# A decoder layer on one core: the first product in token groups of 256, low weights first in each triple, and three operands of the up product at other addresses

## The chip, the core and the metric

The kernel runs on one core of a Trainium2 chip. The core has five engines that run in parallel, each with a queue of its own that it works through in order: TensorE (PE, with its weight loads listed as PEld), VectorE (DVE), ScalarE (ACT), GpSimd (POOL) and SyncE (SP, which here issues DMAs). They wait for each other through semaphores. Data lies in SBUF (128 partitions), TensorE writes its sums to PSUM banks. The metric is the device time of one execution in microseconds (us); before the change the median of three runs is 1292.92 us (1291.68 to 1296.99).

## The reference

One layer of a decoder on 1024 tokens and 16 meta tokens in front of them, model width 1024, all in float32. Cut to what matters:

```python
h = layer_norm(concat(meta_tokens, x))                 # 1040 x 1024
z = h @ w_in + b_in                                    # the first product
q, k, v, c_in, gates = split(z, [512, 128, 128, 1024, 2048])
y_attn = window_attention(q, k, v) @ w_attn_proj       # 8 query heads, 2 key heads, window 128
c_val, c_gate = split(c_in)
c = causal_dwconv(c_val * sigmoid(c_gate), conv_dw)    # 31 taps, 512 channels
y_conv = silu(layer_norm(c)) @ w_conv_proj
mixed = sigmoid(g_attn) * y_attn + sigmoid(g_conv) * y_conv
h = layer_norm(ALPHA * h + mixed @ w_out)
u, g = split(causal_dwconv(h @ ffn_w_up, ffn_dw))      # 3 taps, 2 x 2816 columns
h = layer_norm(ALPHA * h + (gelu(g) * u) @ ffn_w_down)
return h[16:]                                          # without the meta tokens
```

## The kernel before

Matrix products run in a reduced-width form of float32. So that nothing is lost, each operand is split into a high part (the number rounded to that form, written by a cast) and a low part (the rest, written by a subtraction), and a product of 128 rows is made as a **triple** of matmuls into the same PSUM bank: high weights by high operand, high weights by low operand, low weights by high operand. Each matmul has a weight load of its own. In `product()` these are lines 332, 335 and 336. For the tiles that start the first product `z_first()` has the same triple at line 538, and for up line 1502. The weights of a tile of the first product are loaded (SP), cast on ACT (line 300, `whi`) and split on DVE or POOL (line 303, `wlo`), and both go into buffers of a pool with two of each. A weight tile holds 8 blocks of 128 columns, each block padded to `WS` = 144 floats, so a tile is 1152 floats in a partition, and `wlo` lies 1152 floats behind `whi`.

The stages follow each other in this order (times of the profiled execution):

- **0 to 62 us.** The input norm, and beside it the first three tiles of z (k, v and the first quarter of q).
- **62 to 436.5 us: the first product**, 27 further tiles of 128 columns of z. A tile has the transposed h as the moving operand, its high part in RHO and its low part in RHC. The tokens are cut into the groups of `HG`: 272, 384 and 384 (in the tiles of q and of the gates, which leave out part of the meta tokens, the first group, `TG`, has 258). A group is 8 triples into one of three PSUM banks (`ps_z`), which is then cleared: for the convolution's gate by ACT (lines 689 and 690), for its value by DVE into `cin` (line 697), for the 16 merge gates by ACT (line 713) with a store to DRAM behind it. The first tiles are a pair for the convolution (gate, then value), a second pair, and the rest of q; further pairs and the gates follow, mixed with the attention's small matmuls. DVE runs the 31 taps of the convolution for each pair (lines 704 and 706), beside the attention's softmax. Before the taps DVE copies k (`kx`, line 726 and on), the meta values (`vmT`, `vm`) and v (line 758). When the taps of all four chunks are done, DVE adds them up (`csum`, line 919), PE sums over channels with matmuls on it (`ps_m`, line 924), and DVE does the convolution's layer norm.
- **436.5 to 531 us: the projections** (`ps_p`) of attention and convolution, by `product()`, in groups of 258 and three times 256 tokens (`PG`).
- **531 to 629 us**: the product with w_out, in matmuls of 512 columns.
- **629 to 1062 us: up.** 22 chunks. Each chunk is a two-by-two split of the matrices with seven products instead of eight, on sums of quadrants. The seven operands are B11, B21, BT2, BT1, BT3, BT4 and B22, prepared once and used in all chunks; each product has 12 matmuls over 258 tokens (`SUB` 0) and 12 over 256 (`SUB` 1). `B_AT` says where the operands lie: those over 258 tokens B11 at the start of RHC, B21 4096 floats into RHO, the four BT in OA, and B22 at the start of RX.
- **1062 us to the end**: down, the last norm and the output.

The order of instructions on an engine is made when the kernel is built: a scheduler takes the ready instruction of the lowest rank, with modelled times, and `rank()` gives a stretch of code its rank (evacuations of PSUM have `RK_EVAC`, the splits `RK_SPLIT`). A kernel whose groups or costs change therefore has another order, too. On the chip each engine keeps to its order and waits.

Where tiles lie matters to the text. In lines of 64 bytes from the start of a partition, B11, B21 and B22 over 258 tokens begin at 841.5, 1617.5 and 2920.5; in OA, BT4 begins at 2528 and BT1 at 2268 (multiples of 4 lines, 256 bytes), BT2 at 2138 and BT3 at 2398. The products of a chunk follow as B11 (bank `px`), B21 (`pz`), BT2 (`px`), BT4 (`pw`), BT1 (`py`), BT3 (`px`) and B22 (`py`).

Of the kernel before, what the change touches and what calls it, by code (L numbers as in the profile page):

```python
# [52 lines left out]
HG = [(0, 272), (272, 656), (656, 1040)]  # L53
UG = [(0, 386), (386, 770), (770, 1026)]
# [15 lines left out]
W_FLAT = 96  # L70
# [40 lines left out]
def tile_hybrid_layer(  # L111
# [202 lines left out]
    def weights(shape, fill):  # L314
        fills[0] += 1
        n = fills[0]
        own = n == 3
        raw = OB[:, 0:D].rearrange("p (k c) -> p k c", k=KC) if own else wraw(shape)
        with rank({1: 14, 2: 13, 3: 16, 4: 23}.get(n, RK_SPLIT)):
            last_fill.append(fill(raw))  # L320
        hi, lo = ((sp.tile([P, KC, WS], R, name=t + "3") if own else wsp(t))[:, :, :P] for t in ("whi", "wlo"))
        if n <= 3:
            return hi, lo, raw
        with rank(RK_SPLIT):
            last_split.append(split(raw, hi, lo, n <= 23))
        return hi, lo

    def product(ps, terms, behind=None):

        n = len(terms)  # L330
        for i, (ah, al, bh, bl) in enumerate(terms):
            ins = nc.tensor.matmul(ps, ah, bh, start=i == 0, stop=False)  # L332
            if i == 0 and behind is not None:
                after(ins, behind)
            nc.tensor.matmul(ps, ah, bl, start=False, stop=False)  # L335
            last = nc.tensor.matmul(ps, al, bh, start=False, stop=i == n - 1)  # L336
# [16 lines left out]

    TG = [(a + U0 if i == 0 else a, b) for i, (a, b) in enumerate(HG)]

# [168 lines left out]
    def z_first(g, tiles, *ks, raw=False):  # L524
# [5 lines left out]
        for k in ks:  # L530
            for i in tiles:
# [5 lines left out]
                for j, (w, hl) in enumerate(((hi, 0), (hi, 1), (lo, 0))):  # L537
# [145 lines left out]
    def conv_chunk(c):  # L683
# [8 lines left out]
        z_tile(in_cols(10 + c), HG, g_evac, wt_c1 if c == 1 else None)  # L692
# [6 lines left out]
        z_tile(in_cols(6 + c), HG, v_evac2)  # L699
# [368 lines left out]
    def prep_wo(k, raw=None, behind=None):  # L1068
# [4 lines left out]
        else:  # L1073
            hi, lo = (wsp_flat(n) for n in ("whi", "wlo"))
# [11 lines left out]
    W_AT = (2064, 3088, 0, 1024)  # L1086
# [9 lines left out]
    for m in range(KC):  # L1096
# [42 lines left out]
        if m < 4:  # L1139
            early.append(FA[:, W_AT[m]:W_AT[m] + 1024])  # L1140
            after(load(early[m], w_out_v[m]), last_gate)
# [19 lines left out]
    B_AT = [[(RHC, 0), (RHO, 4096)] + [(OA, OA_UP + i * KC * BS[0]) for i in range(4)] + [(RX, 0)],  # L1161
# [153 lines left out]
    def wsplit(src):  # L1315
# [3 lines left out]
        if RING[i] is None:  # L1319
            RING[i] = wsp_flat(("whi", "wlo")[i % 2])  # L1320
# [328 lines left out]
    def ln_rows():  # L1649
        return [wsp_flat(t, F) for t in ("whi", "wlo")]  # L1650
# [130 lines left out]
```

## Time and profile before

| | us |
|---|---|
| median of three runs | 1292.92 |
| profiled execution | 1290.93 |
| span of it on the core | 1289.1 |
| PE busy | 1263.4 (98%) |
| PE weight loads busy | 1189.8 (92%) |
| DVE busy | 1085.9 (84%) |
| ACT busy | 580.3 (45%) |
| POOL busy | 66.4 (5%) |
| first product, from 62 to | 436.5 |
| up, from 629 to | 1062 |
| mean granted clock of TensorE | 0.995 |

A row of the timeline has the start, the duration, the engine, the line, the operation, what it writes and reads, the shape and how many were put together; in brackets stands how long the engine was idle before it and what ended that. Matmuls are pipelined: a duration reaches over the next one's start, so the pace is read from one start to the next. In a table of stretches each engine's busy time is followed by its count of instructions, and behind POOL's stand the granted clock of TensorE, the busy share of the DMA engines and what they moved. A row of a group has its busy time and the mean in ns of one, and then the idle time ahead of it with what ended most of it.

### The profile page before, as it was taken

To read this page: it belongs to the slowest core of one execution; us is meant where nothing else is said; L and a number is where in the kernel's file an instruction comes from. 1 tells how busy PE (TensorE), PEld (TensorE's weight loads), DVE (VectorE), ACT (ScalarE), POOL (GpSimd) and SP (SyncE) were. 2 spreads that over 40 slices of the span, in tenths; PEclk is the share of its full clock that TensorE was granted. 3 is DMA by queue.
4 is the path that set the end of the run, shared out by engine and by line. 5 is a ranking of instruction groups with operands and counts; after the bars stand their busy time and mean duration, and the time that the engine had idled before them with its cause. 6 is when DMAs were issued, how large, how long until landed. Compare 5 with 4: busy or idle time off the path is not lost.

```text
span 1289.1 us, 21679 instructions
## 1 busy us (share of the span) xinstructions
PE 1263.4 (98%) x8546; PEld 1189.8 (92%) x8546; DVE 1085.9 (84%) x1836; ACT 580.3 (45%) x1051; POOL 66.4 (5%) x35
## 2 busy tenths in 40 slices
PE   7999999999999999999999999999999999999997
PEld 7889999999989999788899999999999997888886
DVE  7888999999967777647899999989899886887697
ACT  5423234454547222344664554555545543536330
POOL 2100000001112222100000000000000000000000
PEclk9999999999999999999999999999999999999999
DMA  6274734334243665222235454453455556989722
GB/s 245 83 265 108 185 93 116 100 82 115 67 112 119 201 166 146 92 82 82 83 103 204 173 208 178 182 202 129 161 182 195 196 198 242 393 286 388 260 76 82
DMA packets 96297, 212.11 MB, mean 165 GB/s; under 512 B 11059, under 2 KB 36211, under 8 KB 95938
## 3 DMA queue, kind: packets, MB, share of 16 engines
q1 hardware_dynamic: 84426, 199.64, 46.2%
q10 hardware_dynamic: 11768, 11.08, 2.6%
q8 instruction: 67, 1.10, 0.4%
q14 instruction: 36, 0.29, 0.1%
HBM read 150.29 MB, written 62.70 MB: 165 GB/s over the span
## 4 chain that ended last, share of the span: by engine, by line
PE 80%; DVE 13%; DMA 4%; ACT 1%; issue 1%; SPq 1%; ACTq 0%; POOL 0%; DVEq 0%
PE px L1502 14%; PE py L1502 9%; PE ps_x L1627 9%; PE ps_z L1627 5%; PE ps_z L332 5%; PE ps_z L335 5%; PE ps_z L336 5%; PE pz L1502 5%; PE pw L1502 5%; DVE FA L706 4%; PE ps_p L336 2%; PE ps_p L335 2%; PE ps_p L332 2%; PE ps_w L332 2%; PE ps_w L336 2%; PE ps_w L335 2%
## 5 line engine op out<-in xcount | busy, mean ns | idle before, releaser
L332 PE MATMUL ps_z<-RHO,whi 128*128 128x384 f32 (+2 forms) x648 | 209.8, 324 | 2.6 <-DVE cin L697 2.6
L335 PE MATMUL ps_z<-RHC,whi 128*128 128x384 f32 (+2 forms) x648 | 210.1, 324 | 0.0
L336 PE MATMUL ps_z<-RHO,wlo 128*128 128x384 f32 (+2 forms) x648 | 209.5, 324 | 0.0
L706 DVE SCALAR_TENSOR_TENSOR FA<-cin,cdw,FA 128x1026 f32<-128x1026 f32 x120 | 154.9, 1305 | 0.1
L332 PEld LDWEIGHTS ps_z<-RHO,whi 128*128 128x128 f32 x648 | 122.5, 189 | 3.5 <-DVE cin L697 3.0
L336 PEld LDWEIGHTS ps_z<-RHO,wlo 128*128 128x128 f32 x648 | 122.3, 189 | 1.2 <-issue 0.3
L335 PEld LDWEIGHTS ps_z<-RHC,whi 128*128 128x128 f32 x648 | 122.6, 189 | 0.7
L300 ACT CAST whi<-wr 128x1024 fp32r<-128x1024 f32 x37 | 38.8, 1049 | 75.6 <-PE ps_z L335 58.4
L1324 DVE TENSOR_TENSOR RHO<-wr,RHO 128x512 fp32r<-128x512 f32 x94 | 64.0, 689 | 9.5 <-ACT RHO L1323 9.5
L1323 ACT CAST RHO<-wr 128x512 fp32r<-128x512 f32 x94 | 56.7, 619 | 25.8 <-DVE wr L1341 11.6
L1341 DVE TENSOR_TENSOR wr<-wr 128x512 f32<-128x512 f32 x88 | 60.6, 689 | 0.2
L303 POOL TENSOR_TENSOR wlo<-wr,whi 128x1024 fp32r<-128x1024 f32 x17 | 42.1, 2474 | 187.2 <-ACT whi L300 158.8
L1514 ACT COPY FA<-px 128x514 f32<-128x514 f32 (+2 forms) x23 | 13.1, 571 | 79.0 <-PE px L1502 79.0
L713 ACT ACTIVATE FA<-ps_z,colr 128x384 f32<-128x384 f32 (+1 forms) x48 | 26.0, 542 | 48.4 <-PE ps_z L336 46.4
L1502 PE MATMUL px<-OA,RHO 128*128 128x258 f32 x324 | 43.2, 282 | 0.0
L1429 ACT ACTIVATE FA<-OB,coll 128x512 f32<-128x512 f32 x44 | 35.9, 816 | 15.2 <-DVE OB L1510 15.2
L1502 PE MATMUL px<-OC,RHO 128*128 128x256 f32 x324 | 42.2, 280 | 0.0
L1502 PE MATMUL px<-RHC,RHO 128*128 128x258 f32 (+1 forms) x312 | 40.9, 280 | 0.4 <-ACT OB L1514 0.4
L1514 ACT COPY OB<-px 128x514 f32<-128x514 f32 (+2 forms) x46 | 26.1, 567 | 32.6 <-PE px L1502 32.6
L1502 PEld LDWEIGHTS px<-OA,RHO 128*128 128x128 f32 x324 | 40.5, 189 | 0.2 <-ACT OB L1514 0.2
L880 ACT ACTIVATE s<-s,sm 128x272 f32<-128x272 f32 (+1 forms) x64 | 31.8, 500 | 18.1 <-DVE sm L876 16.3
L1502 PEld LDWEIGHTS px<-OC,RHO 128*128 128x128 f32 x324 | 39.9, 189 | 0.1
(468 smaller groups left out, 3387.2 us busy)
## 6 DMA issues: line engine op xcount, KB each, us to landing
wr<-in_w_up_dram SPq DMA_DIRECT2D x44, 512.0 KB, 4.2
wr<-in_w_z_dram SPq DMA_DIRECT2D x29, 512.0 KB, 4.0
fd<-FA SPq DMA_DIRECT2D x44, 256.0 KB, 2.5
OB<-in_w_down_dram SPq DMA_DIRECT2D x21, 512.0 KB, 4.7
FA<-sd SPq DMA_DIRECT2D x15, 512.0 KB, 8.1
qt<-qd SPq DMA_DIRECT2D x28, 256.0 KB, 4.0
sgd<-FA ACTq DMA_DIRECT2D x32, 192.0 KB, 2.6
td<-OB SPq DMA_DIRECT2D x12, 512.0 KB, 3.2
```

The costliest lines, as they stand in the source:

```text
L300: ins = nc.scalar.copy(hi, raw)
L303: return (nc.vector if quick else nc.gpsimd).tensor_tensor(lo, raw, f32(hi), OP.subtract)
L332: ins = nc.tensor.matmul(ps, ah, bh, start=i == 0, stop=False)
L335: nc.tensor.matmul(ps, ah, bl, start=False, stop=False)
L336: last = nc.tensor.matmul(ps, al, bh, start=False, stop=i == n - 1)
L706: nc.vector.scalar_tensor_tensor(acc[c], cin[:, j:j + U], wc, acc[c], OP.mult, OP.add)
L1323: nc.scalar.copy(hi, src)
L1324: ins = nc.vector.tensor_tensor(lo, src, f32(hi), OP.subtract)
L1341: ins = nc.vector.tensor_tensor(*x)
L1502: ins = nc.tensor.matmul(o, x[:, ks], bmat(sub, q, hl, k), start=first and k + j == 0, stop=k == 3 and j == 2, skip_group_check=not first)
L1514: copied.append(nc.scalar.copy(*x))
L1627: nc.tensor.matmul(banks[i], l[:, ts], r[:, ws], start=first and a and x + k == 0, stop=z and x == len(ops) - 1 and k == 2, skip_group_che ...
```

## The change

Four things are changed together.

1. The 27 later tiles of the first product use `ZG`: token groups of 272 (258 in q and the gates), 256, 256 and 256 instead of 272, 384 and 384. The starting tiles keep `HG`. A group is cleared as before, so each tile has one more clearing, and a merge gate one more store.
2. The triple of `product()` and of `z_first()` begins with low weights by high operand, then high by high, then high by low. Up keeps its order.
3. `whi` and `wlo` become one tile `w` of 2304 floats (pool of two); the low part begins 1136 instead of 1152 floats behind the high one, 64 bytes lower, in the padding behind the last block of the high part. The flat views that later stages take of these buffers have the addresses that they had.
4. Three operands of up over 258 tokens move: B11 by 40 floats, B21 by 40 floats and B22 by 56 floats. They then begin at lines 844, 1620 and 2924.

The rename of `W_AT` to `E_AT` in the w_out stage only frees the name. With item 3's line numbers, 332, 335 and 336 become 341, 342 and 338; 300 and 303 become 302 and 305, 697 becomes 703, 713 becomes 719, 919 and 924 become 925 and 930.

```diff
+ZG = [(0, 272), (272, 528), (528, 784), (784, 1040)]
...
-W_FLAT = 96
+W_AT = (0, 1136)
+W_FLAT = (96, 1136 + 112)
...
-    def wsp(tag, dtype=R):
-        return wsp_p.tile([P, KC, WS], dtype, name=tag, tag=tag)
-
-    def wsp_flat(tag, dtype=R):
-        return wsp(tag, dtype).rearrange("p k c -> p (k c)")[:, W_FLAT:W_FLAT + D]
+    def chunks(t):
+        return [t[:, o:o + KC * WS].rearrange("p (k c) -> p k c", k=KC)[:, :, :P] for o in W_AT]
+
+    def wsp(dtype=R):
+        return wsp_p.tile([P, 2 * KC * WS], dtype, name="w", tag="w")
+
+    def wsp_flat(dtype=R):
+        t = wsp(dtype)
+        return [t[:, o:o + D] for o in W_FLAT]
...
-        hi, lo = ((sp.tile([P, KC, WS], R, name=t + "3") if own else wsp(t))[:, :, :P] for t in ("whi", "wlo"))
+        hi, lo = chunks(sp.tile([P, 2 * KC * WS], R, name="w3") if own else wsp())
...
-            ins = nc.tensor.matmul(ps, ah, bh, start=i == 0, stop=False)
+            ins = nc.tensor.matmul(ps, al, bh, start=i == 0, stop=False)
...
-            nc.tensor.matmul(ps, ah, bl, start=False, stop=False)
-            last = nc.tensor.matmul(ps, al, bh, start=False, stop=i == n - 1)
+            nc.tensor.matmul(ps, ah, bh, start=False, stop=False)
+            last = nc.tensor.matmul(ps, ah, bl, start=False, stop=i == n - 1)
...
-    TG = [(a + U0 if i == 0 else a, b) for i, (a, b) in enumerate(HG)]
+    TG = [(a + U0 if i == 0 else a, b) for i, (a, b) in enumerate(ZG)]
...
-                for j, (w, hl) in enumerate(((hi, 0), (hi, 1), (lo, 0))):
+                for j, (w, hl) in enumerate(((lo, 0), (hi, 0), (hi, 1))):
...
-        z_tile(in_cols(10 + c), HG, g_evac, wt_c1 if c == 1 else None)
+        z_tile(in_cols(10 + c), ZG, g_evac, wt_c1 if c == 1 else None)
...
-        z_tile(in_cols(6 + c), HG, v_evac2)
+        z_tile(in_cols(6 + c), ZG, v_evac2)
...
-    B_AT = [[(RHC, 0), (RHO, 4096)] + [(OA, OA_UP + i * KC * BS[0]) for i in range(4)] + [(RX, 0)],
+    B_AT = [[(RHC, 40), (RHO, 4096 + 40)] + [(OA, OA_UP + i * KC * BS[0]) for i in range(4)] + [(RX, 56)],
             [(OC, OC_UP + i * 2048) for i in range(4)] + [(RHC, 4096 + R_DN), (RHC, 2048 + R_DN), (RHC, 6144 + R_DN)]]
```

More of the change, by code (lines that the diff above doesn't have):

```diff
@@ L1073, in prep_wo @@
         else:
-            hi, lo = (wsp_flat(n) for n in ("whi", "wlo"))
+            hi, lo = wsp_flat()
         if raw is None:
@@ L1085, in tile_hybrid_layer @@
     GS += [(OB, i * 516) for i in range(5)]
-    W_AT = (2064, 3088, 0, 1024)
+    E_AT = (2064, 3088, 0, 1024)
     def gslot():
@@ L1139, in tile_hybrid_layer @@
         if m < 4:
-            early.append(FA[:, W_AT[m]:W_AT[m] + 1024])
+            early.append(FA[:, E_AT[m]:E_AT[m] + 1024])
             after(load(early[m], w_out_v[m]), last_gate)
@@ L1319, in wsplit @@
         if RING[i] is None:
-            RING[i] = wsp_flat(("whi", "wlo")[i % 2])
+            RING[i:i + 2] = wsp_flat()
         t = RING[i]
@@ L1649, in ln_rows @@
     def ln_rows():
-        return [wsp_flat(t, F) for t in ("whi", "wlo")]
+        return wsp_flat(F)
     gains = ln_rows()
```

## The prediction

> **What bounds the kernel now.** I read the busy table first, then the stretches, then the chain of work that ended last. TensorE (PE) is busy 98% of the span, so its own pace and its few waits set the time; but in the first product (62 to 436.5 us) VectorE (DVE) is nearly as full:
>
> ```profile
> PE 1263.4 (98%) x8546; PEld 1189.8 (92%) x8546; DVE 1085.9 (84%) x1836; ACT 580.3 (45%) x1051; POOL 66.4 (5%) x35
> ```
> ```profile
> core 0: us, PE busy (x) PEld busy (x) DVE busy (x) ACT busy (x) POOL busy (x), PEclk, DMA share, GB/s
> 86.00:94.00 8.00, 5.37 (x29) 5.05 (x28) 5.98 (x17) 1.04 (x1) 0.00 (x0) 0.79 0.74 272
> 118.00:215.00 97.00, 95.10 (x622) 94.08 (x622) 90.60 (x152) 34.69 (x84) 0.00 (x0) 1.00 0.48 129
> ...
> 300.00:364.00 64.00, 62.62 (x403) 59.99 (x401) 63.60 (x119) 33.16 (x87) 9.62 (x4) 1.00 0.29 84
> 364.00:436.50 72.50, 72.37 (x444) 70.87 (x445) 53.60 (x108) 36.51 (x59) 12.21 (x5) 1.00 0.50 140
> ```
>
> So there are two questions: what the change does to the pace of the matmuls, and whether DVE lets the first product use it. The pace is read from starts. In the timeline of PE, 5 steps of 272 columns lie between the first two rows below (0.63 us, 126 ns each), 26 of 384 from there to the next (4.52 us, 173.8 ns each), and 22 of 384 between the last two (3.92 us, 178.2 ns each): the same product has two paces.
>
> ```profile
> 64.81 0.29 PE L335 MATMUL ps_z<-RHC,whi 128*128 128x272 f32 x1
> ...
> 65.44 0.34 PE L332 MATMUL ps_z<-RHO,whi 128*128 128x384 f32 x1
> ...
> 69.96 0.34 PE L336 MATMUL ps_z<-RHO,wlo 128*128 128x384 f32 x1
> ...
> 118.01 0.34 PE L336 MATMUL ps_z<-RHO,wlo 128*128 128x384 f32 x1
> ...
> 121.93 0.34 PE L332 MATMUL ps_z<-RHO,whi 128*128 128x384 f32 x1
> ```
>
> 256 columns have two paces as well, at the start of up, where pieces of 12 follow each other without a break:
>
> ```profile
> 629.11 1.58 PE L1502 MATMUL px<-OC,RHO 128*128 128x256 f32 x12
> 630.53 1.58 PE L1502 MATMUL pz<-OC,RHO 128*128 128x256 f32 x12
> 631.94 1.58 PE L1502 MATMUL px<-OC,RHO 128*128 128x256 f32 x12
> ...
> 635.55 1.65 PE L1502 MATMUL pw<-RHC,RHO 128*128 128x256 f32 x12 [0.97 <-ACT FA L1304]
> 637.03 1.52 PE L1502 MATMUL py<-OC,whi 128*128 128x256 f32 x12
> 638.39 1.52 PE L1502 MATMUL px<-RHC,wlo 128*128 128x256 f32 x12
> ```
>
> Between 629.11 and 631.94 lie 24 matmuls: 117.9 ns each. Behind a wait of 0.97 us it is 1.36 us for 12: 113.3 ns. These operands all stand to their weights in the same way in memory (the next weights begin 64 bytes behind the operand, taken modulo 256), so with one placement both paces occur, and the pace seems to be carried on from what ran before. In the projections, 72 steps of 256 columns lie between these two rows, 117.1 ns each:
>
> ```profile
> 450.95 0.29 PE L332 MATMUL ps_p<-OA,whi 128*128 128x256 f32 x1
> ...
> 459.38 0.28 PE L332 MATMUL ps_p<-OA,whi 128*128 128x258 f32 x1
> ```
>
> **The up product.** The chain of waits shows seven products of up in a row (the first closes one chunk, six belong to the next), each 12 matmuls of 258 and 12 of 256 columns (start, us, what):
>
> ```profile
> 946.66 2.86 PE py L1502 x24
> 949.52 2.85 PE px L1502 x24
> 952.37 2.85 PE pz L1502 x24
> 955.22 2.81 PE px L1502 x24
> 958.03 2.81 PE pw L1502 x24
> 960.85 2.81 PE py L1502 x24
> 963.66 2.81 PE px L1502 x24
> ```
>
> The first three are those of B22, B11 and B21, the three operands that are moved; the other four read OA. The moved ones lie half a 64-byte line off a line; among the four, those of pw and py lie on multiples of 256 bytes. After the change the three lie on such multiples too. Were they then to run as pw and py do, they would lose 0.05 + 0.04 + 0.04 = 0.13 us a chunk, times 22 chunks: **-2.9 us**. PE has no wait here that could hide it: it is what the chain runs along. Bounds: nothing changes (0); or the half-line cost is paid in another form. The best 256-column pace, 113.3 against 117.9 ns, bounds the gain: 36 x 4.6 ns x 22 = -3.6. A loss is not excluded by a row; the same 0.13 a chunk the other way, +2.9, bounds it. I take -2.9, since the four products on lines all run at 2.81.
>
> **The first product: more and smaller groups.** Each of the 27 tiles that come after the start has 1040 or 1026 columns; two groups of 384 become three of 256, for 24 matmuls each, so 48 matmuls become 72 in a tile, 648 more in all. What the order does, on PE at the edge of the first two groups, before:
>
> ```order
> L336 MATMUL ps_z<-RHO,wlo 128x272
> L332 MATMUL ps_z<-RHO,whi 128x384
> L335 MATMUL ps_z<-RHC,whi 128x384
> L336 MATMUL ps_z<-RHO,wlo 128x384
> L332 MATMUL ps_z<-RHO,whi 128x384
> ```
>
> and after:
>
> ```order
> L342 MATMUL ps_z<-RHC,w 128x272
> L338 MATMUL ps_z<-RHO,w 128x256
> L341 MATMUL ps_z<-RHO,w 128x256
> L342 MATMUL ps_z<-RHC,w 128x256
> L338 MATMUL ps_z<-RHO,w 128x256
> ```
>
> The low weights have moved ahead of the two high ones. With lo one line lower, every weight load now begins 64 bytes behind the operand being read (modulo 256); before, one in three began 128 behind. That is the placement of the 629 us rows, so 113.3 or 117.9 ns are the prices. A pair of 384s takes 347.6 to 356.4 ns, three 256s 339.9 to 353.7. Times 648: from -10.7 to +4.0 us; the middles (352.0 and 346.8) give **-3.4** of PE work. The same order and placement hold for the 576 matmuls of 256 columns of the projections, at 117.1 now: -2.2 to +0.5, taken as **-0.9**, the middle; they lie on the path (PE 94.5 of 94.5 us from 436.5 to 531).
>
> A rule speaks against all of this. The Trainium skill, "TensorE: Matmul & The Clock Gate", Part 1, "Wait — 56ns, not 53.3ns?", has a fixed cost of about 2.5 ns for each matmul and nothing that depends on addresses; by it 648 matmuls cost 1.6 us more, an estimate from that page, and the moves nothing. The trace disagrees: one size has two paces, 113.3 and 117.9 ns.
>
> **The first product: a wait that goes.** At 86 us PE stands still, the largest wait that it has:
>
> ```profile
> 86.41 0.34 PE L336 MATMUL ps_z<-RHO,wlo 128*128 128x384 f32 x1
> 89.38 0.59 PE L332 MATMUL ps_z<-RHO,whi 128*128 128x272 f32 x1 [2.63 <-DVE cin L697]
> ...
> 92.49 0.41 PE L335 MATMUL ps_z<-RHC,whi 128*128 128x272 f32 x1
> ```
> ```profile
> 86.61 1.04 ACT L300 CAST whi<-wr 128x1024 fp32r<-128x1024 f32 x1 [10.62 <-PE ps_z L335]
> ```
> ```profile
> 87.69 1.23 DVE L303 TENSOR_TENSOR wlo<-wr,whi 128x1024 fp32r<-128x1024 f32 x1 [4.98 <-ACT whi L300]
> 88.83 1.55 DVE L697 SCALAR_TENSOR_TENSOR cin<-ps_z,colr,FA 128x272 f32<-128x272 f32 x3
> ...
> 100.17 0.28 DVE L748 TENSOR_TENSOR vm<-ps_vm,vm 64x128 fp32r<-64x128 f32 x1 [2.71 <-ACT vm L747]
> ...
> 104.08 1.22 DVE L303 TENSOR_TENSOR wlo<-wr,whi 128x1024 fp32r<-128x1024 f32 x1 [2.08 <-ACT whi L300]
> 105.23 0.81 DVE L704 TENSOR_SCALAR FA<-cin,cdw,colr 128x1026 f32<-128x1026 f32 x1
> ```
>
> DVE waits at L303 for a cast on ACT, which waits for a weight buffer that PE still reads; the three evacuations of PE's banks (L697) stand behind L303. PE waits 2.6 us for a bank, and then runs at half pace: from 89.38 to 92.49 lie 13 steps of 239 ns, against 126 for 272 columns at 65 us, 1.5 us more (granted clock 0.79 in 86 to 94). On DVE, before:
>
> ```order
> L303 TENSOR_TENSOR wlo<-wr,whi 128x8x128
> L697 SCALAR_TENSOR_TENSOR cin<-ps_z,colr,FA 128x272
> L697 SCALAR_TENSOR_TENSOR cin<-ps_z,colr,FA 128x384 x2
> L726 CAST kx_758<-FA 128x8x128
> L726 CAST kx_758<-FA 128x8x16
> ```
>
> and after, the end of the same stretch, behind three evacuations that now come early:
>
> ```order
> L748 COPY vmT<-FA 64x16 x4
> L703 SCALAR_TENSOR_TENSOR cin<-ps_z,colr,FA 128x256
> L305 TENSOR_TENSOR w<-wr,w 128x8x128
> L754 TENSOR_TENSOR vm<-ps_vm,vm 64x2x64
> L764 TENSOR_TENSOR v<-ps_v_794,v 128x4x64 x2
> ```
>
> This split (now L305) has sunk from ahead of the evacuations to behind all four, so the circle of waits opens. The fourth evacuation is queued behind the work on kx and vmT; the tile's next user of that bank comes three groups on, so I leave PE about 1 us of wait there (an estimate: some 7 us of kx and vmT work from 90.29 on against two groups of 2.8). On PE that is 2.6 + 1.5 - 1.0, a gain of **3.1 us**. DVE's three waits above add up to 9.8 us; I let 1.8 stand, so DVE reaches the first tap of the convolution (L704) about 8 us sooner.
>
> **What the first product can keep.** From that tap on DVE carries the taps (L706) and the attention until csum, for which PE waits:
>
> ```profile
> 361.11 2.96 DVE L919 TENSOR_TENSOR csum<-csum,FA 128x1026 f32<-128x1026 f32 x1
> ```
> ```profile
> 362.41 0.28 PE L335 MATMUL ps_z<-RHC,whi 128*128 128x258 f32 x1
> 364.13 1.35 PE L924 MATMUL ps_m<-csum,ones 128*128 128x386 f32 x4 [1.44 <-DVE csum L919]
> ...
> 436.65 0.28 PE L332 MATMUL ps_p<-OA,whi 128*128 128x258 f32 x1
> ```
>
> PE's order puts a fixed amount of the product behind csum, so the product's end is csum plus 72 us. On PE there, before:
>
> ```order
> L900 MATMUL ps_o<-pl,v 128x512
> L336 MATMUL ps_z<-RHO,wlo 128x258
> L332 MATMUL ps_z<-RHO,whi 128x258
> L335 MATMUL ps_z<-RHC,whi 128x258
> L924 MATMUL ps_m<-csum,ones 128x386
> L924 MATMUL ps_m<-csum,ones 128x256
> ```
>
> and after:
>
> ```order
> L338 MATMUL ps_z<-RHO,w 128x256
> L930 MATMUL ps_m<-csum,ones 128x386
> L930 MATMUL ps_m<-csum,ones 128x384
> L930 MATMUL ps_m<-csum,ones 128x256
> L341 MATMUL ps_z<-RHO,w 128x256
> L342 MATMUL ps_z<-RHC,w 128x256
> ```
>
> It stands after 516,976 columns of z instead of 522,630: PE comes there 2.6 us of work sooner, faster matmuls and no stall sooner still, so DVE decides. DVE gets 4 more evacuations into cin and one more into qsl, the columns being the same: some 1.3 us in all, an estimate from the 1.55 us that three take above. Four pieces of attention of some 0.65 us (two each of L892 and L826) now stand ahead of csum as well: 2.6. So csum comes at -8 + 3.9 = -4.1, and the 72 us behind it, a fifth of the product, run 0.5 sooner at the middle pace: **-4.6** for the whole of the first product, stall and pace together. With DVE 0 or 10 us sooner it is +3.4 to -6.6. ACT's 16 more gate evacuations and 16 more stores are covered: ACT mostly waits for PE there (46.4 us).
>
> ```profile
> L713 ACT ACTIVATE FA<-ps_z,colr 128x384 f32<-128x384 f32 (+1 forms) x48 | 26.0, 542 | 48.4 <-PE ps_z L336 46.4
> ```
>
> **Sum.** -2.9 - 0.9 - 4.6 = -8.4 against the profiled execution's 1290.9 (span 1289.1 and 1.8 around it): 1282.5. The median of the runs lies 2.0 above the profiled one, so **1284.5**.
>
> **Rivals.** (1) DVE gains less than it seems: v and the splits still wait for ACT, the taps start only 4 us sooner or less, and the 3.9 us of work moved ahead of csum eat it. With 4 us z gives nothing and -3.8 stays, 1289; with 0 it is +3.4 in z, 1292.5. For it: DVE's 63.6 of 64 us ahead of csum. Against: the evacuations have left the circle. (2) Placement does nothing and each matmul has a price of its own: up and the projections give 0; z costs PE up to the +4.0 above, of which a fifth, 0.8, lies behind csum; DVE's -4.1 stands: about 1290. The two paces of 256 columns speak against it. The Trainium skill (same page, Part 2, "Step-by-step: what each phase is for") has two independent read ports for the moving operand and the weights, which would make it so. (3) Slower: four groups share three banks, and a group lasts 2.8 us instead of 4.2, so a bank must be cleared within 5.6 instead of 8.4 us; DVE clears between taps in a fixed order, and PE waits at every group. 108 groups at 0.2 us are 21.6 us: about 1306. It decides from 0.14 us a group (14.9 us over the forecast). For it: the wait at 86 us is of this kind. Against: the 1.44 us at csum is of another kind, and 80 of the groups are cleared by ACT, which waits for PE.
>
> **How the numbers follow.** Forecast 0.59, rival 1 0.20, rival 2 0.08, rival 3 0.13. Half a per cent, 6.5 us, is about what a measurement can tell from no change: below 1286.5 is faster, above 1299.4 slower. The forecast lies 2 us inside; what of it falls into "no change" and what of the rivals falls into "faster" about cancel: faster 0.60, same 0.27, slower 0.13. Range: from -3.6 - 2.2 - 6.6 (1280.5), less 3 for a z that gains on PE beyond what DVE's 10 us allow, up to rival 1 with DVE no sooner: 1277.5 to 1293. Rival 3 and a little below are left out.
>
> **What would show it.** Right: all seven products of up at 2.81; no wait at L338 or L341 for cin above 1 us and the clock near 1.00 in 86 to 94; the first tap near 97 to 100; csum ending near 360 and the projections starting near 432; 256 columns of z at or near 113 ns. Wrong: B11, B21 or B22 still at 2.85; first tap after 104; many small waits of ps_z for L703 or L719; a wait at csum so long that the clock halves behind it as at 89.

## The result: no change that can be measured, and a first product that got slower inside

Over twelve runs of each, the changed kernel takes 1293.69 us (1289.78 to 1295.46), the kernel before 1294.59 (1290.98 to 1296.99). The ratio is 0.9993, with a 95% interval of 0.9982 to 1.0004. Forecast were 1284.5 us and a range of 1277.5 to 1293.

The profile of the changed kernel is of an execution of 1293.89 us (span 1292.1). Its busy table and its stretches have this in place of the lines shown of before:

```profile
PE 1261.5 (98%) x9194; PEld 1189.1 (92%) x9194; DVE 1089.0 (84%) x1843; ACT 589.8 (46%) x1082; POOL 65.7 (5%) x35
```
```profile
core 0: us, PE busy (x) PEld busy (x) DVE busy (x) ACT busy (x) POOL busy (x), PEclk, DMA share, GB/s
86.00:94.00 8.00, 5.11 (x42) 4.91 (x41) 3.89 (x12) 1.05 (x1) 0.00 (x0) 1.00 0.99 320
94.00:118.00 24.00, 21.64 (x168) 21.67 (x169) 20.03 (x29) 6.67 (x14) 0.00 (x0) 0.86 0.56 142
118.00:215.00 97.00, 93.73 (x788) 93.27 (x788) 86.37 (x151) 38.11 (x96) 0.00 (x0) 0.96 0.46 121
...
300.00:364.00 64.00, 64.00 (x518) 62.43 (x518) 63.32 (x105) 30.87 (x78) 10.28 (x4) 1.00 0.32 91
364.00:436.50 72.50, 68.73 (x567) 66.98 (x567) 59.07 (x108) 38.76 (x63) 14.75 (x6) 1.00 0.53 142
```

PE's busy time is 1.9 us less although it does 648 matmuls more, but in the first product idle gaps have opened, in 86 to 118, in 118 to 215 and, new, in 364 to 436.5 us. By the first starts in each stage, the stages lasted (us):

| stage | before | before, second profile | changed | changed, second profile |
|---|---|---|---|---|
| first product | 374.2 | 376.0 | 379.8 | 375.7 |
| projections and w_out | 192.5 | 192.5 | 191.4 | 191.5 |
| up | 439.1 | 438.8 | 436.9 | 437.4 |
| down and the end | 220.9 | 220.8 | 220.7 | 221.0 |

The profile before that the prediction started from was a short execution; the second one (e0 below) is 2.1 us longer, nearly all of it in the first product. So one profile of this kernel is good to some 2 us in that stage, and to a few tenths in the others; the two profiles of the changed kernel differ by 4.1 us in it. A steadier estimate comes from the medians: they differ by 0.9 us, and the projections and up together gained 2.4 to 3.3 us in the table, so the first product of the changed kernel is some 2 us longer, an estimate.

Up's products run as predicted. In the chain of waits of the changed kernel all seven now take the same time:

```profile
832.45 2.81 PE py L1508 x24
835.26 2.81 PE px L1508 x24
838.08 2.81 PE pz L1508 x24
840.89 2.81 PE px L1508 x24
843.70 2.81 PE pw L1508 x24
846.52 2.81 PE py L1508 x24
849.33 2.81 PE px L1508 x24
```

The pace in the first product came as well. Between these two starts in the timeline of PE lie 72 steps of 256 columns, 115.4 ns each:

```profile
121.29 0.28 PE L338 MATMUL ps_z<-RHO,w 128*128 128x256 f32 x1
...
129.60 0.28 PE L338 MATMUL ps_z<-RHO,w 128*128 128x258 f32 x1
```

Where the time went are PE's waits. The first stands where the old one was, and is twice as long; the next two are for the queries' data, with half clock behind them (from 161.17 to 164.15 lie 14 steps of 213 ns); the fourth was not there before:

```profile
90.83 0.28 PE L342 MATMUL ps_z<-RHC,w 128*128 128x256 f32 x1
96.36 0.39 PE L751 MATMUL ps_vm<-coll,vmT 128*64 128x128 f32 x1 [5.25 <-DVE vmT L748]
...
157.20 0.17 PE L790 MATMUL ps_s<-kx,qt 128*2 128x16 f32 x1 [1.58 <-DMA qt<-qd]
...
160.38 0.17 PE L790 MATMUL ps_s<-kx,qt 128*2 128x16 f32 x1 [1.69 <-DMA qt<-qd]
...
161.17 0.41 PE L338 MATMUL ps_z<-RHO,w 128*128 128x256 f32 x1
...
164.15 0.41 PE L342 MATMUL ps_z<-RHC,w 128*128 128x256 f32 x1
...
391.97 0.39 PE L338 MATMUL ps_z<-RHO,w 128*128 128x256 f32 x1 [2.54 <-ACT FA L719]
```

Added up over the first product from the starts on PE, in us (pace: for each width, the mean of the undisturbed steps, those under 1.25 times the median, times their number; waits: gaps above 0.15 us; drag: what the product's own matmuls took above their pace and these waits, half clock and interruptions):

| | before | changed | second of before | second of changed |
|---|---|---|---|---|
| pace of the product's matmuls | 307.8 | 304.2 | 307.8 | 304.1 |
| attention and other matmuls | 52.9 | 52.0 | 53.0 | 52.0 |
| waits | 6.0 | 12.3 | 6.3 | 11.0 |
| drag | 7.5 | 11.4 | 8.9 | 8.6 |

3.6 us of pace were gained, as predicted (3.4), and 4 to 10 us of waits and drag came in their place. No wait for cin is left at 89 us and the clock in 86 to 94 us is 1.00, as the prediction asked; the wait stands at the next matmul that DVE feeds.

DVE shows why the first wait came back. It clears three groups early, as predicted, and then stands still 3.9 us between the first and the second pair of k copies; the profile names no releaser ("issue"). The last of eight stores of x, issued at 82.20, lands at 89.69 us by the trace, 0.08 us before the copies go on; in the second profile it lands at 90.38 and they go on at 90.46. vmT and the fourth clearing of cin are queued behind that:

```profile
85.03 0.82 DVE L732 CAST kx<-FA 128x1024 fp32r<-128x1024 f32 x2
89.77 0.83 DVE L732 CAST kx<-FA 128x1024 fp32r<-128x1024 f32 x2 [3.92 <-issue]
...
95.49 0.72 DVE L748 COPY vmT<-FA 64x16 f32<-64x16 f32 x4
96.24 0.48 DVE L703 SCALAR_TENSOR_TENSOR cin<-ps_z,colr,FA 128x256 f32<-128x256 f32 x1
...
102.39 0.82 DVE L710 TENSOR_SCALAR FA<-cin,cdw,colr 128x1026 f32<-128x1026 f32 x1 [3.06 <-PE ps_v L759]
```

The first tap is 2.8 us sooner than before (3.5 in the second pair of profiles), not 8. And PE meets vm's transposes sooner: in its order they stand behind 57,984 columns of the first product, before behind 68,736.

Behind csum, ACT switches its function table between the layer norm (L984, L996) and the gates (L719), 1.28 us each time, and the gate that PE waits for stands behind such a switch:

```profile
389.10 1.03 ACT L302 CAST w<-wr 128x1024 fp32r<-128x1024 f32 x1
390.15 1.28 ACT L719 ACT_TABLE_LOAD   x1
391.44 0.84 ACT L719 ACTIVATE FA<-ps_z,colr 128x256 f32<-128x256 f32 x2
...
392.79 1.28 ACT L984 ACT_TABLE_LOAD   x1 [0.50 <-ACT FA L719]
...
394.58 1.28 ACT L996 ACT_TABLE_LOAD   x1
```

csum comes later in this pair of profiles, and the projections follow 75.5 us behind it instead of 72.5, in both pairs. The two waits for ACT (2.54 and 0.52 us) are this difference: 5,654 more columns of the product stand behind csum (1.7 us) and 11 fewer other matmuls (1.8 us), which cancel:

```profile
367.58 2.00 PE L930 MATMUL ps_m<-csum,ones 128*128 128x386 f32 x6 [0.71 <-DVE csum L925]
...
443.11 0.28 PE L338 MATMUL ps_p<-OA,w 128*128 128x258 f32 x1
```

### The profile page after: what moved, and what is told of

The parts are those of the page before. It is cut to its first block, busy times and chain, and to the rows that moved or that the text cites. A ratio compares the mean times of both kernels' runs of the same rounds, so it can differ in the third digit from the quotient of the medians.

```text
span 1292.1 us, 23058 instructions
## 1 busy us (share of the span) xinstructions
PE 1261.5 (98%) x9194; PEld 1189.1 (92%) x9194; DVE 1089.0 (84%) x1843; ACT 589.8 (46%) x1082; POOL 65.7 (5%) x35
## 4 chain that ended last, share of the span: by engine, by line
PE 77%; DVE 14%; DMA 3%; ACT 2%; issue 2%; SPq 1%; POOL 0%; DVEq 0%; ACTq 0%
PE px L1508 14%; PE py L1508 9%; PE ps_x L1633 9%; PE ps_z L1633 5%; PE pz L1508 5%; PE pw L1508 5%; DVE FA L712 4%; PE ps_z L342 4%; PE ps_z L338 4%; PE ps_z L341 4%; PE ps_p L342 2%; PE ps_p L338 2%; PE ps_p L341 2%; PE ps_w L342 2%; PE ps_w L338 2%; PE ps_w L341 2%
## 5 line engine op out<-in xcount | busy, mean ns | idle before, releaser
L338 PE MATMUL ps_z<-RHO,w 128*128 128x256 f32 (+2 forms) x864 | 245.9, 285 | 3.1 <-ACT FA L719 3.1
L341 PE MATMUL ps_z<-RHO,w 128*128 128x256 f32 (+2 forms) x864 | 246.4, 285 | 0.0
L342 PE MATMUL ps_z<-RHC,w 128*128 128x256 f32 (+2 forms) x864 | 245.5, 284 | 0.0
L338 PEld LDWEIGHTS ps_z<-RHO,w 128*128 128x128 f32 x864 | 164.5, 190 | 4.2 <-ACT FA L719 2.7
L342 PEld LDWEIGHTS ps_z<-RHC,w 128*128 128x128 f32 x864 | 164.6, 190 | 0.6
L341 PEld LDWEIGHTS ps_z<-RHO,w 128*128 128x128 f32 x864 | 164.6, 190 | 0.5
L712 DVE SCALAR_TENSOR_TENSOR FA<-cin,cdw,FA 128x1026 f32<-128x1026 f32 x120 | 158.1, 1325 | 0.5
L302 ACT CAST w<-wr 128x1024 fp32r<-128x1024 f32 x37 | 38.8, 1048 | 65.1 <-PE ps_z L342 45.1
L719 ACT ACTIVATE FA<-ps_z,colr 128x258 f32<-128x258 f32 (+1 forms) x64 | 30.1, 471 | 52.1 <-PE ps_z L342 44.3
L305 POOL TENSOR_TENSOR w<-wr,w 128x1024 fp32r<-128x1024 f32 x17 | 42.2, 2484 | 188.6 <-ACT w L302 179.8
L1330 DVE TENSOR_TENSOR w<-wr,w 128x512 fp32r<-128x512 f32 x60 | 40.6, 685 | 4.9 <-ACT w L1329 4.7
L1329 ACT CAST w<-wr 128x512 fp32r<-128x512 f32 x60 | 36.4, 619 | 14.1 <-DVE wr L1347 6.4
```

Source lines behind the costliest of these rows:

```text
L302: ins = nc.scalar.copy(hi, raw)
L305: return (nc.vector if quick else nc.gpsimd).tensor_tensor(lo, raw, f32(hi), OP.subtract)
L338: ins = nc.tensor.matmul(ps, al, bh, start=i == 0, stop=False)
L341: nc.tensor.matmul(ps, ah, bh, start=False, stop=False)
L342: last = nc.tensor.matmul(ps, ah, bl, start=False, stop=i == n - 1)
L712: nc.vector.scalar_tensor_tensor(acc[c], cin[:, j:j + U], wc, acc[c], OP.mult, OP.add)
```

## The experiments

My theory after the two traces: the gains of pace are real and belong to placement; the four groups change the order on PE, DVE and ACT, and the waits of the new order eat what they and the placement gain. The rival: DVE alone sets the end of the first product, whatever PE does. The ratios below are to runs of the kernel before on the same chip.

### e0: the kernel before, again

> The kernel before once more, for a second profile. If the profile shown before the prediction is typical, the projections start within 1 us of 436.65 and csum ends within 1 us of 364.07. If it was a lucky one (the median of twelve runs is 1294.59, it took 1290.93), the first product ends some 3 us later and the other stages last as long as they did.

It took 1293.02 us; csum came 2.5 us later and the projections at 439.2. The profile before was a lucky one, as the second branch has it. The two differ in the wait for the queries' data (1.5 and 1.9 us) and in whether the clock halved behind it: by the drag worked out as above, 1.5 us from 158.55 to 162 in the second, none in the first.

### e1: the three operands of up alone

```diff
-    B_AT = [[(RHC, 0), (RHO, 4096)] + [(OA, OA_UP + i * KC * BS[0]) for i in range(4)] + [(RX, 0)],
+    B_AT = [[(RHC, 40), (RHO, 4096 + 40)] + [(OA, OA_UP + i * KC * BS[0]) for i in range(4)] + [(RX, 56)],
```

> Only the three operands of up are moved. Theory (the cost is placement, each product at 2.81 us): up shortens by 2.2 us as in the changed kernel's profile, all else as before, 1292.4 against 1294.6. Rival (up's gain in the changed kernel comes from the state in which the earlier stages leave TensorE): up stays, 1294.6.

1290.31 us against 1294.3, ratio 0.9975 (0.9965 to 0.9986). Up lasted 436.9 instead of 439.1 us, all other stages as before. The gain is placement, it needs nothing of the other parts, and its size is as in the changed kernel.

### e2: the four groups alone

```diff
+ZG = [(0, 272), (272, 528), (528, 784), (784, 1040)]
...
-    TG = [(a + U0 if i == 0 else a, b) for i, (a, b) in enumerate(HG)]
+    TG = [(a + U0 if i == 0 else a, b) for i, (a, b) in enumerate(ZG)]
...
-        z_tile(in_cols(10 + c), HG, g_evac, wt_c1 if c == 1 else None)
+        z_tile(in_cols(10 + c), ZG, g_evac, wt_c1 if c == 1 else None)
...
-        z_tile(in_cols(6 + c), HG, v_evac2)
+        z_tile(in_cols(6 + c), ZG, v_evac2)
```

> Only the four groups in the first product; old order of the triple and old placement. Theory (the groups bring an order on TensorE in which the transposes for vm stand about 9,000 columns of work earlier, ahead of data that DVE has only at 96 us): a wait of about 4 us at ps_vm, half clock behind it, and ACT as in the changed kernel late at a gate; the pace of 256 columns stays near 117.3 (351.9 for three against 353.4 for two of 384, -1.0 us in all); total 3 to 6 us slower than before. Rival (DVE alone sets the end of the first product): slower by the 2.6 us of extra work on DVE, with the waits on TensorE absorbed.

```profile
96.36 0.27 PE L746 MATMUL ps_vm<-coll,vmT 128*64 128x128 f32 x1 [2.31 <-DVE vmT L743]
```

1295.65 us, ratio 1.0012 (0.9999 to 1.0024): no more than a tendency to slower. The first product lasted 378.0 us. A step of 256 columns took 117.7 ns here (mean of all, interruptions left out), so without the placement the groups are worth little; the wait at vm is there (2.31 us), and so are the waits for gates (1.96 and 1.02 us). Theory and rival both expected slower; the theory's 3 to 6 us were too much, and the run doesn't decide between them.

### e3: low weights first and lower, with the old groups

The changed kernel with the old groups, and with `B_AT` as before:

```diff
-    TG = [(a + U0 if i == 0 else a, b) for i, (a, b) in enumerate(ZG)]
+    TG = [(a + U0 if i == 0 else a, b) for i, (a, b) in enumerate(HG)]
...
-        z_tile(in_cols(10 + c), ZG, g_evac, wt_c1 if c == 1 else None)
+        z_tile(in_cols(10 + c), HG, g_evac, wt_c1 if c == 1 else None)
...
-        z_tile(in_cols(6 + c), ZG, v_evac2)
+        z_tile(in_cols(6 + c), HG, v_evac2)
```

> Low weights first and 64 bytes lower, but the old groups, and up's operands as before. Theory (placement sets the pace, and waits set the rest): 384 columns fall from 176.7 to 170 to 174 ns, -3.5 to -8.7 us of TensorE work in the first product; the projections -0.9; as transposes for vm stand only 1,900 columns earlier than before, the wait for them is short, and 3 to 6 us are gained. Rival (DVE sets the end of the first product): only the projections' 0.9 us.

1288.10 us, ratio 0.9955 (0.9942 to 0.9969). The gain is in the theory's range, but not for its reason: 384 columns went only from 176.7 to 176.3 ns. The pace of the whole first product, reckoned as above, fell by 0.8 us (307.8 to 307.0; the groups of 258 columns went from 119.9 to 118.9 ns), its waits from 6.0 and 6.3 to 5.2, its drag from 7.5 and 8.9 to 6.8, and PE no longer waited for csum; the projections' matmuls went from 117.3 to 115.6 ns. What 170 to 174 ns assumed, that 384 columns would follow the same rule as 256, is refuted. Most of the gain on PE is thus fewer waits and less drag, in an order that differs again; why they fell was not tested, and no run takes the order of the triple apart from the 64 bytes.

### e5: vm's transposes where they stood before

`after` makes its first instruction stand behind its second in the order, and `z_last` holds the last matmul of each group of `product()` in the first product.

```diff
-    nc.tensor.transpose(ps[:64, :P], vmT, ident)
+    vm_turn = nc.tensor.transpose(ps[:64, :P], vmT, ident)
...
...
     conv_chunk(1)
     conv_chunk(0)
+    after(vm_turn, z_last[10])
```

> The changed kernel with one order added: PE's transposes for vm stay behind 68,736 columns of the first product, where they stood before, instead of 57,984. Theory (this order made the 5.25 us wait): the wait falls under 1 us and the half clock from 96 to 100 us goes, about 6 us of PE time ahead of csum; DVE reaches the first tap 1 to 2 us sooner, so csum and the end come 1 to 3 us sooner, 1291 to 1293. Rival (each wait on PE adds to the whole): 6 us, 1288. Second rival (DVE sets the end alone, from the k copies on): no change, 1293.7.

1291.78 us, ratio 0.9983 (0.9972 to 0.9995). The wait at vm went and came back as one of 3.25 us for the fourth clearing of cin, one instruction further down DVE's queue:

```profile
97.36 0.39 PE L338 MATMUL ps_z<-RHO,w 128*128 128x256 f32 x1 [3.25 <-DVE cin L704]
```

So the theory's "under 1 us" fails: the place on PE made the wait longer (5.25 against 3.25 us) but was not its cause. DVE was late. The intervals of this ratio and the changed kernel's overlap, so a gain from the place alone isn't shown.

### e4: the merge gates in three groups

```diff
-        z_tile(in_cols(14 + i), TG, gate_evac)
+        z_tile(in_cols(14 + i), [(a + U0 if i == 0 else a, b) for i, (a, b) in enumerate(HG)], gate_evac)
```

> The changed kernel with the 16 merge gates back to three groups (258, 384, 384). Theory (four clearings of a gate come between ACT's table loads for the layer norm, and PE waits for a bank at 389 and 397): these two waits, 3.1 us, go, the pace of the gates costs 16 x 24 x 4.7 ns = 1.8 us, so 1 to 2 us faster than the changed kernel, 1292. Rival (the wait belongs to ACT's order behind csum with any groups): 2 us slower, 1295.5.

1289.63 us over seven runs (1285.83 to 1293.10), ratio 0.9968 (0.9953 to 0.9982). Behind csum one wait of 0.74 us was left of the two. The profile is of the longest of the seven executions (1293.10), and its first product lasted 377.8 us, within the changed kernel's two. By the medians the gates' fourth group costs more here than its pace brings; e11 below doesn't bear that out.

### e7: 4 of 31 taps left out

```diff
-            for j in range(TAPS):
+            for j in range(TAPS - 4):
```

> The changed kernel without 4 of the 31 taps in each chunk of the convolution (left out: 16 of 120 multiply-adds on DVE, about 21 us of its work ahead of csum). Theory (DVE's work sets csum and with it the end of the first product): csum some 15 us sooner, the first product at least 5 us shorter. Rival (waits in PE's and ACT's order set it, DVE has room): csum sooner, but the first product within 2 us of 379.8.

One run, 1287.48 us. In the rows of its timeline csum starts 15.8 us sooner than in the changed kernel, and the projections 6.1 us sooner:

```profile
350.54 1.23 DVE L925 TENSOR_TENSOR csum<-csum,FA 128x1026 f32<-128x1026 f32 x1
```
```profile
436.98 0.28 PE L338 MATMUL ps_p<-OA,w 128*128 128x258 f32 x1
```

The first product lasted 373.0 us, 2.7 to 6.8 less than in the two profiles of the changed kernel. So DVE's work counts, but of 21 us on it at most a third reaches the end: with csum 14 us sooner PE has more of its own product left behind it (171,336 columns against 150,560). "The end is csum plus 72 us", on which the prediction rested, does not hold when csum moves far: from csum's matmuls on PE (353.4) it is 83.6 us here.

### e8: the change without its groups

e3, but with the change's `B_AT` (e1's line).

> The change without its four groups: low weights first and lower, and up's operands moved, groups of 272, 384 and 384. Theory (the two gains lie in different stages and add): e1's ratio 0.9975 and e3's 0.9955 give 0.993, about 1285.3. Rival (a state of TensorE that one leaves is what the other also gives): no more than e3, 1288.5.

1286.00 us, ratio 0.9943 (0.9931 to 0.9955). The gains of e1 and e3 add, within their intervals. The two placements alone beat both kernels. The old wait at cin is still there:

```profile
89.80 0.56 PE L338 MATMUL ps_z<-RHO,w 128*128 128x272 f32 x1 [2.81 <-DVE cin L703]
```

### e9: e8, with the split behind the evacuations

`values` holds the clearings into cin in their order.

```diff
             last_split.append(split(raw, hi, lo, n <= 23))
+            if n == 7:
+                after(last_split[-1], values[2])
```

> e8 with one order added: DVE's split of the weights for the fourth convolution tile stands behind the three evacuations into cin, as the prediction had it. Theory (the waits at 86 to 97 us follow from the copies of k, whose data is in SBUF only at about 89.7 us; taking the split away from the evacuations frees PE, which then runs ahead to the next data from DVE): the wait of 2.8 us at 87 and the half clock behind it go (4.3 us of PE), a new wait of 1 to 3 us comes at vm or at a fourth group, csum moves by less than 2 us, total 0 to 2 us below e8. Rival (the predicted step was right for the old groups): 4 us below e8, 1282.

1282.79 us over four runs, ratio 0.9917 (0.9903 to 0.9932); 3.2 us less than e8 by the medians, though each was measured beside its own set of runs of the kernel before, and the two intervals just touch. The rival is nearer: the step that the prediction took from the groups, the split behind the evacuations, brings about what it said (3.1 us on PE) when it is made by itself, as far as two chips can be compared. PE's wait there fell from 2.81 to 0.55 us and csum came 3.1 us sooner (359.8 against 362.9):

```profile
96.83 0.27 PE L754 MATMUL ps_vm<-coll,vmT 128*64 128x128 f32 x1 [0.55 <-DVE vmT L751]
```
```profile
87.37 0.62 DVE L706 SCALAR_TENSOR_TENSOR cin<-ps_z,colr,FA 128x384 f32<-128x384 f32 x1 [3.27 <-PE ps_z L344]
88.38 1.23 DVE L305 TENSOR_TENSOR w<-wr,w 128x1024 fp32r<-128x1024 f32 x1 [0.39 <-ACT w L302]
```

With three groups the last value group is cleared and the split done before DVE comes to the k copies, at 89.5 us. With four groups the fourth clearing falls behind these copies. The last store of x lands at 88.49 us here, so the split covers the wait for it again. The end gained less in this profile, of the longest of the four executions, than csum (projections at 434.2 against 434.7).

### e10: the k copies behind the fourth evacuation

e5, and all four k copies on DVE (`k_copies`) after the fourth clearing of cin:

```diff
     after(vm_turn, z_last[10])
+    for x in k_copies:
+        after(x, values[3])
```

> e5 (the changed kernel with vm's transposes late) and the copies of k behind the fourth evacuation into cin. Theory (DVE stands waiting for k's data from 86 to 89.7 us with that evacuation behind it): PE's waits between 86 and 100 us fall from 5.25 and 3.25 us to under 1, half clock none; total 3 to 5 us below the changed kernel, 1289 to 1291. Rival (the time returns as a longer wait at csum and at the queries' data near 155 us): 1 us below e5's 1291.8 or no change.

1287.08 us over four runs, ratio 0.9941 (0.9924 to 0.9958), better than the theory's range. PE's waits between 86 and 100 us shrank to one of 1.10 us; the wait at csum (0.53) and those for the queries' data (0.99 and 1.75) grew no longer. So these waits on PE can be taken out without coming back elsewhere, and the changed kernel gains some 6 us. DVE itself still stood still, now for another store, but that ended sooner and less stood between it and the fourth clearing:

```profile
89.11 0.07 DVE L702 MEMSET cin<- 128x16 f32 x1 [3.42 <-DMA v1d<-vrow]
```

### e11: e10, and the gates in three groups

e10 with e4's line.

> e10 with the merge gates in three groups (e4). All three new waits are then out: theory, as the sum of e10 and of what e4 gave (4 us by medians, 2 by the two profiles), 1286 to 1288, and the four groups in the remaining tiles are worth no more than e8 has without them. Rival (four groups in convolution and queries still pay): below e8, 1284.

1288.71 us, ratio 0.9962 (0.9947 to 0.9976). Neither expectation holds: nothing was added to e10. Both first products lasted the same (373.3 and 373.6 us); the gates' pace costs 1.5 us (304.2 to 305.7), and the waits and the drag together are 1.6 us less. e4's gain therefore isn't a fixed price of the fourth gate group, and what e4 gained over the changed kernel beside the gates stays open.

### e12: the changed kernel, again

> The changed kernel once more, for a second profile. The waits at 91 (5.25 us), 155 to 160 (3.3) and 389 (2.5) are in its order, so they come again within 1 us each, and the first product lasts 378 to 381 us. If they were chance, some of them are missing and it lasts 375 or less.

1291.24 us. The first and the last wait came again to 0.04 us; those for the queries' data fell from 3.3 to 2.0 us, and the half clock behind them didn't occur:

```profile
97.05 0.39 PE L751 MATMUL ps_vm<-coll,vmT 128*64 128x128 f32 x1 [5.29 <-DVE vmT L748]
```
```profile
388.51 0.39 PE L338 MATMUL ps_z<-RHO,w 128*128 128x256 f32 x1 [2.54 <-ACT FA L719]
```

The first product, 375.7 us, is shorter than I expected. The waits at 91 and 389 us belong to the order; the length of those near 157 us varies from run to run.

### e13: x's rows 7 stored first

```diff
-    for src, mu, rs, n, j in later:
+    for src, mu, rs, n, j in sorted(later, key=lambda x: x[4] != 7):
...
-        nc.vector.memset(cin[:, 0:16], 0.0)
+        ins = nc.vector.memset(cin[:, 0:16], 0.0)
+        if c == 0:
+            after(ins, vm_copy[-1])
```

> The changed kernel with x's rows 7 normalized and stored ahead of the other rows, and the second clearing of cin behind the copies of vmT. In the changed kernel the second pair of k copies writes where x's rows 7 lie, whose store is the last of eight of 512 KB, and the second clearing of cin where vrow lies. Theory (DVE's 3.9 us of waiting at 86 to 90 us is for that store): the wait in front of the second pair of k copies falls from 3.9 to under 1 us, vmT is ready 3 to 4 us sooner than 96.2, PE's wait for vm falls from 5.3 to 1 to 2 us, and the kernel takes 3 to 5 us less than the changed kernel, 1289 to 1291. Rival (DVE waits for the load of k itself, which the stores only delay): the 3.9 us stay, and the time too.

1286.26 us, ratio 0.9934 (0.9919 to 0.9948): 0.6% under the changed kernel's ratio, more than the theory's 3 to 5 us, by a kernel with the same groups and placement. All four k copies run without a gap, and PE's wait at vm is 1.03 us:

```profile
85.70 1.56 DVE L735 CAST kx<-FA 128x1024 fp32r<-128x1024 f32 x4
...
88.76 0.27 DVE L677 MEMSET vm<- 64x256 f32 x1 [1.27 <-DMA h0d<-x]
...
93.32 0.72 DVE L751 COPY vmT<-FA 64x16 f32<-64x16 f32 x4
...
99.34 0.81 DVE L713 TENSOR_SCALAR FA<-cin,cdw,colr 128x1026 f32<-128x1026 f32 x1 [2.14 <-DMA cdw<-in_cols_dram]
```
```profile
94.18 0.27 PE L754 MATMUL ps_vm<-coll,vmT 128*64 128x128 f32 x1 [1.03 <-DVE cin L701]
```

So DVE's unnamed 3.9 us were the wait for a buffer: the second pair of k copies writes where x's rows 7 lie, and those were still being stored, as the last of eight stores of 512 KB with the DMA engines 99% busy (86 to 94 us in the changed kernel). The load of k isn't it: its two DMAs were issued at 76.9 and 78.1 us here, 0.2 us later than in the changed kernel, and the copies ran at once. A wait of 1.27 us for another store of x is left. The first product lasted 370.9 us, as short as in the best of the kernels with three groups.

### e14: the same in e9

> e9 with the same two moves. Theory (in e9 the split fills the time in which DVE would wait, and PE's wait for vm is 0.55 us already): the first tap at most 1 us sooner and the time within 1 us of e9, 1282 to 1283. Rival (DVE's waits still set e9's csum): 2 to 3 us less, 1280.

1286.12 us, ratio 0.9931 (0.9914 to 0.9947), against e9's 0.9917 (0.9903 to 0.9932). No gain: csum came sooner (356.9 against 359.8), the first product lasted 370.9 against 371.3 us. The theory's 1282 to 1283 is missed, its median lies 3.3 us above e9's, while the runs of the kernel before that stood beside it lie 1.4 us higher too; the intervals of the two ratios overlap, so which of the two is faster stays open. In the two profiles the difference lies in up (438.1 against 436.4 us), which the two moves don't touch.

e9 is the fastest of all by its median; e13 shows what the change as it is could have had.

## Why the prediction was wrong, point by point

**What bounds the kernel: half right.** PE's pace and its waits set the time, and DVE is the second bound of the first product. But "DVE decides, and the end is csum plus 72 us" was too simple: behind csum the waits for ACT put another 3 us in, and with csum 14 us sooner (e7) the first product gained half of that or less.

**Up, -2.9: right in kind, too large.** The stage lost 2.2 us in the changed kernel's first profile, 1.4 in its second and 1.9 in e1 against the second of before. From chunk to chunk it is 19.81 us before and 19.69 after, 0.12 us and not 0.13, and only in the last 20 of the 22 chunks, which makes 2.4 us; in the second profile single stalls took 0.7 us of it back.

**Projections, -0.9: right.** 117.3 to 115.6 ns for 576 matmuls is 1.0 us, and the stage with w_out is 1.0 to 1.1 us shorter.

**Pace in the first product, -3.4: right.** It is 3.6 us: three steps of 116.0 ns in place of two of 176.7, 648 times. The size came out by some luck: undisturbed groups of 24 ran at 115.0 or 116.6 ns a step, not at the 113.3 or 117.9 ns whose middle was taken.

**"A wait that goes", 3.1 us on PE and 8 us on DVE: this is the step that failed.** The order was read right: the split did sink behind the evacuations. Two things were missed. DVE had a second reason to stand still at the same time, hidden in the profile before: the store of x's rows 7 landed at 87.90 us, just behind the end of DVE's wait of 4.98 us at the split (87.69), so the k copies behind it started at 90.29 without a wait. Take the first away and the second shows; store these rows first and it goes (e13). And vm's transposes had moved 10,752 columns of the product ahead on PE, some 5 us of work, so that PE met DVE's vmT before it was ready. I compared the place of ps_m in PE's order and not that of ps_vm. Where the sum left PE 1.0 us of wait, it waited 5.25 us at vm, with half clock behind it again, and with vm's transposes put back still 3.25 us for the fourth clearing (e5). Of the 8 us by which the first tap was to come sooner, 2.8 and 3.5 came.

**csum at -4.1: wrong by this step.** It came 3.5 us later in the first pair of profiles and 2.5 us sooner in the second pair (364.1 against 366.6). By the mean of the two it is half a microsecond later, which the spread hides. It fits that the 2.8 to 3.5 us that DVE gained at the first tap are no more than the 3.9 us of work that the prediction itself had moved ahead of csum; these 3.9 were not measured by themselves.

**"ACT's evacuations are covered": wrong.** The cover was read from ACT's total, 46 us of waiting for PE. At 389 us it is gone, because layer norm and gates alternate, each change of function loads a table, and the gate's clearing that PE needs stands behind such a load. PE waits 2.5 us, in both profiles. The four groups are what uncovers it: e2, which has only them, has the waits, and e3, with the old groups and as many loads (12), has none.

**The rivals.** The first one, that DVE gains less than it seems, had 0.20 and gave 1289 to 1292.5; with DVE 2.8 to 3.5 us sooner it is nearest to what happened, plus the 3 us at the gates that it didn't have. The second fell with e1 and e3: placement pays. By the fixed cost of each matmul that the prediction cites from the Trainium skill ("TensorE: Matmul & The Clock Gate", Part 1, "Wait — 56ns, not 53.3ns?"), 648 more matmuls should take 1.6 us more, an estimate from that page. The trace doesn't agree: with the groups alone (e2) the pace of the product's matmuls went from 307.8 to 307.4 us. The third was wrong in size (two waits, not one a group), right in kind: the wait for ACT at 389 us is for a bank that is cleared late.

**The base.** The profiled execution was 3.7 us below the median of twelve runs, where three had it at 2.0.

## What to carry to other kernels

When a wait is about to go, list what the waiting engine does next and what each of those instructions needs, its output buffer too: the time at which a store or load frees that buffer is a second wait hiding behind the first, and a row that starts just as it ends shows no gap. Where a change re-orders work, compare the place of every matmul that another engine feeds, not only of the one that the sum names. Take placement and grouping apart when a change holds both: here the placement, with low weights first, gave 0.57% by itself, and the groups gave it back until the waits that they brought were removed.

## What the runs showed of the hardware

- The same matmul has several paces, and which one it has depends on where its operands lie: with the three operands moved by 160 or 224 bytes, seven products of up all took 2.81 us instead of four of them (e1). It depends on more than that: the projections' 256 columns, whose lines e2 leaves as they were, took 118.3 ns there and 117.3 before.
- The widths gain differently: with low weights first and 64 bytes lower, 384 columns went from 176.7 to 176.3 ns (e3), 256 columns from 117.3 to 115.6 in the projections and from 117.7 (e2) to 116.0 in the first product, and 272 columns got slower, from 125.3 to 126.7. I had expected a common rule.
- The waits of 2.6 and 5.25 us on PE were followed by some microseconds at half clock (granted clock 0.79 in 86 to 94 us before, 0.86 in 94 to 118 after). Shorter waits halved the clock only in some executions: behind 1.58 and 1.69 us in the changed kernel it did (0.50 from 160.4 to 165.7), behind 0.44 and 1.58 in its second profile it didn't; behind a single wait of 1.92 us it did (e0, 0.51 from 158.5 to 162), behind one of 2.16 us at the same place it didn't (e1, 1.00). So the length of the wait alone doesn't decide. A rule of the Trainium skill bears on it, "TensorE: Matmul & The Clock Gate", Part 1, "What's actually happening": a free-running window of about 3.4 us sets the clock, and the throttled state comes after an idle window. The trace agrees for the wait of 5.25 us; waits of 1.92 to 2.63 us, shorter than that window, halved it as well, and that they do so only at times would fit a window whose phase varies, but no run here shows the window itself.
